# A transformer layer on one core: the opening loads spread over two queues, and the first norm's squares placed behind its last scaled tile

## Chip, core and metric

The kernel runs on one core of one Trainium2 chip. The metric is device time in microseconds (us) of one execution. Five engines work beside each other, each through its own instructions in order: PE (TensorE, matrix products), DVE (VectorE), ACT (ScalarE), POOL (GpSimd) and SP (SyncE, which here only issues transfers). A transfer can be issued by SP or by ACT; the issuing instruction stands in that engine's order like any other, and whatever follows it there comes after it.

## What is computed

One encoder layer on 512 tokens of width 1024, in float32. The part at the beginning is a normalisation and a gated feed-forward half step:

```python
def rms_norm(x, g):
    y = x * lax.rsqrt(jnp.mean(x * x, axis=-1, keepdims=True) + EPS)
    return y * g

def swiglu(h, w_gate, w_up, w_down):
    return (jax.nn.silu(h @ w_gate) * (h @ w_up)) @ w_down

x = x + 0.5 * swiglu(rms_norm(x, ffn1_norm), ffn1_w_gate, ffn1_w_up, ffn1_w_down)
x = x + token_mixing(rms_norm(x, mix_norm), ...)          # gated linear attention and a short convolution
x = x + memory_cross_attention(rms_norm(x, xattn_norm), rms_norm(mem, mem_norm), ...)
x = x + 0.5 * swiglu(rms_norm(x, ffn2_norm), ffn2_w_gate, ffn2_w_up, ffn2_w_down)
out = rms_norm(x, final_norm)
```

The feed-forward width is 2816, so gate and up have 22 tiles of 128 columns each.

## The kernel before

The residual is held transposed, as eight tiles `x[0..7]` of 128 channels by 512 tokens (256 KB each). A norm is split in two: `Norm.scale(d)` multiplies tile d by the gain at once, and the factor 1/rms is multiplied in later, where the products leave PSUM. To keep float32 accuracy each operand of a product is held as a high part and a low part, and a product takes three matmuls (L69 to L71: high by high, high by low, low by high). ACT makes the high part and DVE the low part: of an activation tile in `scaled_split` (`xh` L123, `xl` L124), of a weight unit in `wsplit` (`whi` L65, `wlo` L66). A weight unit is one tile of 128 columns over all 1024 rows, 128x1024 or 512 KB; `ga0`, `ua0`, `ga1`, `ua1` are the first two tiles of gate and up of the first half step. Raw units have four buffers, their high and low parts three each.

The feed-forward loop over f (22 steps, L241) accumulates `pg` (gate) and `pu` (up) over the eight tiles k of the residual, 24 matmuls each. For f = 0 the order is k by k, gate and up in turn, since the tiles arrive one after the other; from f = 1 on it is all of gate, then all of up. The order in which the instructions of an engine finally stand is set by a scheduler from the order in the program and from priorities; the weight units loaded through `unit` have a priority ahead of it.

At the start SP issues everything (`first_units`, L201): residual tiles and quarters of `ga0` and `ua0` (128x256, two k each) in turn, and the scheduler puts `ga1` and `ua1` whole in between. ACT and DVE split them in the same turn.

The sum of squares of the first norm is formed beside that: ACT squares each tile (`Norm.square`, L178: tile 0 into `ssq_n`, L180, the others into `sq_n`, L183, which has two buffers), and POOL adds each square to `ssq_n` (L184, seven adds of 128x512). At f = 2 four small matmuls `rt_n` turn `ssq_n` into the mean over channels, and `rstd_n` comes from it; only then can `finish` empty the banks of f = 0, 1 and 2.

Every transfer signals one of eight semaphores, taken in turn; the ninth transfer's issue waits until the first has landed, and so on. Such waits are named `DMAHW0` to `DMAHW7` below.

Of the kernel before, what the change touches and what calls it, by code (L numbers as in the profile page):

```python
# [15 lines left out]
P = 128  # L16
T = 512
D = 1024
# [12 lines left out]
def layer_kernel(ctx: ExitStack, tc: tile.TileContext, t: dict, outT: bass.AP):  # L31
# [19 lines left out]

# [1 line left out]
    def unit(src, n, name):  # L53
# [19 lines left out]

    # small products, one at a time between the large ones, so that their weights load behind those
    pend = []
# [9 lines left out]
    def mm_cols(ps, w, x, ks, first=True, last=True, tok=slice(0, T)):  # L85
        """ps += the columns of unit w times x; ks: pairs (tile of the unit, tile of x)."""
        whi, wlo = w
        for n, (kw, kx) in enumerate(ks):
            c = slice(kw * P, (kw + 1) * P)
            mm3(ps, whi[:, c], wlo[:, c], x[kx][0][:, tok], x[kx][1][:, tok],  # L90
                first and n == 0, last and n == len(ks) - 1)

    ALL = [(k, k) for k in range(KD)]

# [1 line left out]
    ones = const.tile([P, P], F32, name="ones")  # L96
    nc.gpsimd.memset(ones, 1.0)
    mhalf = const.tile([P, 4], F32, name="mhalf")
    nc.gpsimd.memset(mhalf, -0.5)
    # load the first table and raise the PE's clock while the first tiles are on their way  # L100
    first_table = small.tile([P, 4], F32, tag="warm", name="first_table", bufs=1)
# [20 lines left out]
    def scaled_split(src, g, hi, lo):  # L122
        nc.scalar.activation(hi, src, AF.Copy, scale=g)  # L123
        nc.vector.scalar_tensor_tensor(lo, src, g, hi.bitcast(F32), ALU.mult, ALU.subtract)  # L124

# [1 line left out]
    def rstd_tok(sq, n, width, name):  # L127
        """[128 tokens, n]: the token on the partitions; sq: the tile, or tiles that add up."""
        ps = bank(f"rt_{name}")
        r = small.tile([P, n], F32, tag="rt", name=f"r_{name}", bufs=3)  # L130

        def one(i, m):
            nc.tensor.matmul(ps[:, i:i + 1], lhsT=sq[m][:, i * P:(i + 1) * P], rhs=ones[:, 0:1],
                             start=(i == 0 and m == 0), stop=(i == n - 1 and m == len(sq) - 1), skip_group_check=True)

        def rest():
            ms = small.tile([P, n], F32, tag="ms", name=f"ms_{name}")
            nc.vector.tensor_scalar(ms, ps[:, 0:n], 1.0 / width, EPS, ALU.mult, ALU.add)
            nc.gpsimd.tensor_tensor(r, ms, mhalf[:, 0:n], ALU.pow)

        todo = [[lambda i=i, m=m: one(i, m) for i in range(n)] for m in range(len(sq))]
        todo[-1].append(rest)
        return r, todo

    def spread(r, n, name, parts=2):
        """[128, n * 128] in PSUM: the token on the free axis, the same on every partition."""
        flush()
# [19 lines left out]
    class Norm:  # L167
        """x * gain goes on, split, at once; the factor 1 / rms follows where the products leave PSUM."""

# [4 lines left out]
        def scale(self, d):  # L174
            if self.gi != GFIN:
                scaled_split(x[d], gains[:, self.gi, d:d + 1], xs[d][0], xs[d][1])

        def square(self, d):  # L178
            if d == 0:
                nc.scalar.activation(self.ssq, x[d], AF.Square)  # L180
            else:
                sq = tmp.tile([P, T], F32, tag="sq", name=f"sq_{self.name}{d}", bufs=2)
                nc.scalar.activation(sq, x[d], AF.Square)  # L183
                nc.gpsimd.tensor_tensor(self.ssq, self.ssq, sq, ALU.add)  # L184

        def add(self, d):
# [13 lines left out]

# [1 line left out]
    DOWN = ((0, 8), (8, 15), (15, KF))  # L202

    def first_units(wgu, norm):
        """the first two units and the residual, in the order in which the products need them"""
        g, u = unit(None, D, "ga0"), unit(None, D, "ua0")
        for k in range(0, KD, 2):
            c = slice(k * P, (k + 2) * P)
            for d in (k, k + 1):
                nc.sync.dma_start(x[d], t["xT"][d * P:(d + 1) * P, :])  # L210
                if d == k:
                    nc.sync.dma_start(g[0][:, c], wgu[0, 0][:, c])
                else:
                    nc.sync.dma_start(u[0][:, c], wgu[0, 1][:, c])
        for k in range(0, KD, 2):
            c = slice(k * P, (k + 2) * P)
            norm.scale(k)
            wsplit(*g, c)
            wsplit(*u, c)
            norm.scale(k + 1)  # L220
        return g[1:], u[1:]

    def ffn(wgu, wd, norm, nxt, name, first=None):
# [18 lines left out]
        for f in range(KF):  # L242
            pg, pu = bank(f"pg_{name}{f}"), bank(f"pu_{name}{f}")
            if f == 0 and first is not None:
                g, u = first
                for k in range(KD):
                    mm_cols(pg, g, xs, [(k, k)], k == 0, k == KD - 1)
                    mm_cols(pu, u, xs, [(k, k)], k == 0, k == KD - 1)
                for d in range(KD):
                    norm.square(d)  # L250
            else:
                if f == wait:
                    norm.tok()
                mm_cols(pg, unit(wgu[f, 0], D, f"g{name}{f}"), xs, ALL)
                flush()
                mm_cols(pu, unit(wgu[f, 1], D, f"u{name}{f}"), xs, ALL)
                if f == wait:
                    rstd = norm.rows()
            waiting.append((f, pg, pu))
            if rstd is not None:  # L260
                for w in waiting:
                    finish(*w)
                waiting = []
# [12 lines left out]
    def finale(us, hs):  # L276
        """the last tile of the residual and the last norm, in halves of the tokens"""
        last = KD - 1
# [4 lines left out]
        for i, tok in enumerate(toks):  # L283
            # the residual times the gain, two tiles of it side by side
            y = [tmp.tile([P, T], F32, tag=("fa", "fb", "fs", "fh")[d], name=f"y{d}_{i}") for d in range(KD // 2)]
# [37 lines left out]

# [1 line left out]
    win = t["win"]  # L325
# [23 lines left out]

    # masks over [m, c] of 128 tokens: same chunk and c >= m (forward), c <= m (backward)  # L350
    mf = const.tile([P, P], F32, name="mf")
# [6 lines left out]
    nc.gpsimd.memset(mb[64:128, 0:64], 0.0)  # L358
    # 0 where a chunk's running sum starts anew
    rst = big("rst")  # L360
# [3 lines left out]

    # v and z, tokens on partitions: first columns 0..255 of v, then the others and z
    VK = {0: (256, 4), 1: (288, 3)}
# [35 lines left out]
    def qk(dst, key, j, sc):  # L402
        """each head on both halves of the partitions: forward, backward"""
        ps = bank(f"{key}ps{j}")
# [17 lines left out]

    # gates: rows 0..63 of a head's tile forward, rows 64..127 backward
    lgs, ts = [], []
    for h in range(H):
# [8 lines left out]
        ts.append(ta)  # L434
    # one function at a time: each change of function loads a table
    exps = [nc.scalar.activation(ts[h], ts[h], AF.Exp, scale=-1.0) for h in range(H)]
# [35 lines left out]

# [1 line left out]
    FW, BW = slice(0, 64), slice(64, 128)  # L474
    osn = [None] * H

    def gla(h):
# [33 lines left out]
        for i in range(4):  # L511
            c = slice(i * P, (i + 1) * P)
            for half, r in enumerate((FW, BW)):
                nc.tensor.matmul(aps[half][:, c], lhsT=kin[h][r, c], rhs=qin[h][r, c],
                                 start=(i == 0), stop=(i == 3), skip_group_check=True)
        # the forward triangle over the backward one, the diagonal with the sum of both
        def put(mask, src):
# [39 lines left out]

# [1 line left out]
    rstd2 = big("rstd2")  # L559
# [26 lines left out]

# [1 line left out]
    mk = []  # L588
# [59 lines left out]
    def skewed(gens, lag):  # L648
        """steps of successive generators, each started lag steps after the one before"""
        gens, live, n = list(gens), [], 0  # L650
# [48 lines left out]

# [1 line left out]
    sc = small.tile([P, 4], F32, tag="sc", name="sc", bufs=1)  # L701
# [95 lines left out]

# [1 line left out]
    nf = Norm(GFIN, "nf")  # L799
# [4 lines left out]
def _cols(w):  # L804
    """[K, N] -> [N / 128, 128, K]: a unit is a tile of columns, K in tiles of 128 partitions."""
    k, n = w.shape
    return w.reshape(k // P, P, n // P, P).transpose(2, 1, 0, 3).reshape(n // P, P, k)


def _rows(w, g):  # L810
    """[K, N] -> [K / (128 g), 128, g N]: a unit is g tiles of rows."""
    k, n = w.shape
# [51 lines left out]
```

## Time and profile before

| | us |
|---|---|
| median of 3 runs | 1152.45 (1152.05 to 1152.57) |
| span of the profiled execution, first to last instruction | 1150.4 |
| what lies around that span, against the median | 2.05 |
| PE busy | 1118.1 (97%) |
| PEld (weight loads, beside PE) busy | 934.3 (81%) |
| DVE busy | 576.9 (50%) |
| ACT busy | 392.0 (34%) |
| POOL busy | 173.9 (15%) |

For the profiled execution only its span is given; the runs' times also hold what lies before the first and behind the last instruction. Times of rows below count from the span's start. A busy share is an average over stages with different limits: what the beginning is worth has to be read from the beginning.

### The profile page before, as it was taken

Reading aid. Unit: us, or ns where it says so; the run is one execution under the profiler, and the core shown is the slowest. Engines: PE = TensorE matmul, PEld = TensorE weight load, DVE = VectorE, ACT = ScalarE, POOL = GpSimd, SP = SyncE. Lnnn points to the kernel's source line nnn. Section 1 sums busy time; section 2 is a strip of 40 time slices with the busy share of each in tenths; the row PEclk is TensorE's granted clock in tenths of the full one; section 3 lists DMA queues with packets and bytes.
Section 4 is the critical chain, followed back from the end, with each engine's and each line's share of the span. In section 5 each row is a group of like instructions: output and inputs, shape, how many; then the busy total and the mean of one; then the engine's idle time right before and its main releaser. Section 6 shows DMA issues by size and latency. Waiting matters only on the chain.

```text
span 1150.4 us, 13140 instructions
## 1 busy us (share of the span) xinstructions
PE 1118.1 (97%) x5326; PEld 934.3 (81%) x5326; DVE 576.9 (50%) x735; ACT 392.0 (34%) x549; POOL 173.9 (15%) x145
## 2 busy tenths in 40 slices
PE   8999999999999997798999999999999999999997
PEld 6888888888888986687887888888888888888886
DVE  6455455442333459855767445464555455442223
ACT  6332332322223284322334344353332332232221
POOL 4111111010111027211111300031111011000110
PEclk9999999999999999999999999999999999999998
DMA  6322222323333312311333322032222322323312
GB/s 218 113 95 98 100 92 94 106 85 101 101 95 124 109 56 64 101 56 57 128 104 117 105 79 74 19 128 92 92 92 93 109 92 92 105 83 101 101 51 74
DMA packets 34252, 109.08 MB, mean 95 GB/s; under 512 B 4080, under 2 KB 7152, under 8 KB 34192
## 3 DMA queue, kind: packets, MB, share of 16 engines
q1 hardware_dynamic: 34048, 108.23, 28.8%
q8 instruction: 41, 0.67, 0.2%
q14 instruction: 19, 0.16, 0.0%
q10 hardware_dynamic: 144, 0.02, 0.0%
HBM read 106.14 MB, written 2.10 MB: 94 GB/s over the span
## 4 chain that ended last, share of the span: by engine, by line
PE 86%; DVE 7%; issue 3%; ACT 1%; POOL 1%; DMA 1%; SPq 0%; POOLq 0%; DVEq 0%; ACTq 0%
PE pg_b L69 4%; PE pg_b L71 3%; PE pd_a L69 3%; PE pu_b L71 3%; PE pu_b L69 3%; PE pg_b L70 3%; PE pd_a L71 3%; PE pd_a L70 3%; PE pu_b L70 3%; PE pu_a L71 3%; PE pu_a L70 3%; PE pu_a L69 3%; PE pg_a L69 3%; PE pg_a L70 3%; PE pg_a L71 3%
## 5 line engine op out<-in xcount | busy, mean ns | idle before, releaser
L71 PE MATMUL pu_a<-xh,wlo_ua 128*128 128x512 f32 x176 | 68.7, 390 | 1.3 <-DVE wlo_ua L66 1.3
L71 PE MATMUL pg_a<-xh,wlo_ga 128*128 128x512 f32 x176 | 68.7, 391 | 0.6 <-DVE wlo_ga L66 0.6
L69 PE MATMUL pg_a<-xh,whi_ga 128*128 128x512 f32 x176 | 69.2, 395 | 0.0
L70 PE MATMUL pg_a<-xl,whi_ga 128*128 128x512 f32 x176 | 68.9, 392 | 0.1
L69 PE MATMUL pg_b<-xh,whi_gb 128*128 128x512 f32 x176 | 68.8, 391 | 0.0
L69 PE MATMUL pu_a<-xh,whi_ua 128*128 128x512 f32 x176 | 68.6, 390 | 0.0
L70 PE MATMUL pg_b<-xl,whi_gb 128*128 128x512 f32 x176 | 68.5, 389 | 0.0
L70 PE MATMUL pu_a<-xl,whi_ua 128*128 128x512 f32 x176 | 68.5, 389 | 0.0
L71 PE MATMUL pg_b<-xh,wlo_gb 128*128 128x512 f32 x176 | 68.5, 389 | 0.0
L71 PE MATMUL pu_b<-xh,wlo_ub 128*128 128x512 f32 x176 | 68.5, 389 | 0.0
L69 PE MATMUL pd_a<-hh_a,whi_da 128*128 128x512 f32 x176 | 68.5, 389 | 0.0
L70 PE MATMUL pd_a<-hl_a,whi_da 128*128 128x512 f32 x176 | 68.5, 389 | 0.0
L71 PE MATMUL pd_a<-hh_a,wlo_da 128*128 128x512 f32 x176 | 68.5, 389 | 0.0
L69 PE MATMUL pu_b<-xh,whi_ub 128*128 128x512 f32 x176 | 68.5, 389 | 0.0
L70 PE MATMUL pu_b<-xl,whi_ub 128*128 128x512 f32 x176 | 68.5, 389 | 0.0
L69 PE MATMUL pd_b<-hh_b,whi_db 128*128 128x512 f32 x154 | 59.9, 389 | 0.0
L70 PE MATMUL pd_b<-hl_b,whi_db 128*128 128x512 f32 x154 | 59.9, 389 | 0.0
L71 PE MATMUL pd_b<-hh_b,wlo_db 128*128 128x512 f32 x154 | 59.9, 389 | 0.0
L235 POOL TENSOR_TENSOR fh_a<-fs_a,fb_a 128x512 f32<-128x512 f32 x22 | 30.8, 1402 | 186.5 <-DVE fb_a L233 155.6
L235 POOL TENSOR_TENSOR fh_b<-fs_b,fb_b 128x512 f32<-128x512 f32 x22 | 28.4, 1292 | 198.9 <-DVE fb_b L233 182.2
L66 DVE TENSOR_TENSOR wlo_db<-raw_db,whi_db 128x896 fp32r<-128x896 f32 (+1 forms) x24 | 29.3, 1220 | 54.8 <-ACT whi_db L65 54.2
L66 DVE TENSOR_TENSOR wlo_da<-raw_da,whi_da 128x896 fp32r<-128x896 f32 (+1 forms) x24 | 28.4, 1182 | 49.8 <-ACT whi_da L65 49.1
(361 smaller groups left out, 2773.3 us busy)
## 6 DMA issues: line engine op xcount, KB each, us to landing
raw_gb<-in_w2gu SPq DMA_DIRECT2D x22, 512.0 KB, 3.5
raw_ub<-in_w2gu SPq DMA_DIRECT2D x22, 512.0 KB, 3.4
raw_ga<-in_w1gu SPq DMA_DIRECT2D x21, 512.0 KB, 3.5
raw_ua<-in_w1gu SPq DMA_DIRECT2D x21, 512.0 KB, 3.4
raw_da<-in_w1d SPq DMA_DIRECT2D x16, 448.0 KB, 3.3
raw_db<-in_w2d SPq DMA_DIRECT2D x16, 448.0 KB, 3.2
raw_da<-in_w1d SPq DMA_DIRECT2D x8, 512.0 KB, 3.5
raw_wk<-in_wk SPq DMA_DIRECT2D x8, 512.0 KB, 3.6
```

What stands on the lines that cost most here:

```text
L66: nc.vector.tensor_tensor(lo[:, c], raw[:, c], hi[:, c].bitcast(F32), ALU.subtract)
L69: nc.tensor.matmul(ps, lhsT=whi, rhs=xhi, start=start, stop=False)
L70: nc.tensor.matmul(ps, lhsT=whi, rhs=xlo, start=False, stop=False)
L71: nc.tensor.matmul(ps, lhsT=wlo, rhs=xhi, start=False, stop=stop)
L235: nc.gpsimd.tensor_tensor(h, s, b, ALU.mult)
```

## The change

- `first_units` now opens `ga0`, `ua0`, `ga1` and `ua1` itself and lets ACT issue their loads: first the two heads (columns for k = 0 and 1, 128x256), then the two rests (128x768), then `ga1` and `ua1` whole. All of them are written ahead of ACT's first split.
- SP loads the eight residual tiles one after the other, with nothing between them.
- The splits are written in a new order: tile 0, both heads, tiles 1 and 2, both rests, tiles 3 and 4, `ga1`, tiles 5 and 6, `ua1`, tile 7.
- f = 1 uses the units opened here and is written k by k like f = 0.
- The eight squares are all tied behind the last scaled split (`xh` of tile 7) in ACT's order.

```diff
     def scaled_split(src, g, hi, lo):
-        nc.scalar.activation(hi, src, AF.Copy, scale=g)
+        i = nc.scalar.activation(hi, src, AF.Copy, scale=g)
         nc.vector.scalar_tensor_tensor(lo, src, g, hi.bitcast(F32), ALU.mult, ALU.subtract)
+        return i
...
-        def square(self, d):
+        def square(self, d, behind=None):
             if d == 0:
-                nc.scalar.activation(self.ssq, x[d], AF.Square)
+                i = nc.scalar.activation(self.ssq, x[d], AF.Square)
             else:
                 sq = tmp.tile([P, T], F32, tag="sq", name=f"sq_{self.name}{d}", bufs=2)
-                nc.scalar.activation(sq, x[d], AF.Square)
+                i = nc.scalar.activation(sq, x[d], AF.Square)
                 nc.gpsimd.tensor_tensor(self.ssq, self.ssq, sq, ALU.add)
+            if behind is not None:
+                after(i, behind)
...
     def first_units(wgu, norm):
-        g, u = unit(None, D, "ga0"), unit(None, D, "ua0")
-        for k in range(0, KD, 2):
-            c = slice(k * P, (k + 2) * P)
-            for d in (k, k + 1):
-                nc.sync.dma_start(x[d], t["xT"][d * P:(d + 1) * P, :])
-                if d == k:
-                    nc.sync.dma_start(g[0][:, c], wgu[0, 0][:, c])
-                else:
-                    nc.sync.dma_start(u[0][:, c], wgu[0, 1][:, c])
-        for k in range(0, KD, 2):
-            c = slice(k * P, (k + 2) * P)
-            norm.scale(k)
-            wsplit(*g, c)
-            wsplit(*u, c)
-            norm.scale(k + 1)
-        return g[1:], u[1:]
+        units = [unit(None, D, n) for n in ("ga0", "ua0", "ga1", "ua1")]
+        head = slice(0, 2 * P)
+        rest = slice(2 * P, D)
+        for c in (head, rest):
+            for n in range(2):
+                nc.scalar.dma_start(units[n][0][:, c], wgu[0, n][:, c])
+        for d in range(KD):
+            nc.sync.dma_start(x[d], t["xT"][d * P:(d + 1) * P, :])
+        for n in range(2):
+            nc.scalar.dma_start(units[2 + n][0], wgu[1, n])
+        norm.scale(0)
+        for n in range(2):
+            wsplit(*units[n], head)
+        norm.scale(1)
+        norm.scale(2)
+        for n in range(2):
+            wsplit(*units[n], rest)
+        for d in range(3, KD):
+            norm.scale(d)
+            if d in (4, 6):
+                wsplit(*units[d // 2], slice(0, D))
+        return [u[1:] for u in units]
...
-            if f == 0 and first is not None:
-                g, u = first
+            if f < 2 and first is not None:
+                g, u = first[2 * f:2 * f + 2]
                 for k in range(KD):
                     mm_cols(pg, g, xs, [(k, k)], k == 0, k == KD - 1)
                     mm_cols(pu, u, xs, [(k, k)], k == 0, k == KD - 1)
-                for d in range(KD):
-                    norm.square(d)
+                if f == 0:
+                    for d in range(KD):
+                        norm.square(d, norm.scaled)
```

What the scheduler makes of it differs from the program's order, so three places are shown as the engines get them. From f = 2 on, the instructions of every engine stand in the same order as before.

**ACT, the first instructions.** Before, from the end of the warm-up (`onesr`) on:

```order
L107 ACTIVATE onesr_93<-ones_76 128x128
L123 ACTIVATE xh0_111<-x0_103,gains_100 128x512 [waits DMAHW1_49,DMAHW0_49]
L65 ACTIVATE whi_ga0_130<-raw_ga0_129 128x256 [waits DMAHW2_49]
L180 ACTIVATE ssq_n1_128<-x0_103 128x512
L123 ACTIVATE xh1_113<-x1_104,gains_100 128x512 [waits DMAHW3_49]
```

Now, from the same instruction on:

```order
L107 ACTIVATE onesr_93<-ones_76 128x128
L214 DMA raw_ga0_129<-in_w1gu 128x256
L214 DMA raw_ua0_132<-in_w1gu 128x256
L214 DMA raw_ga0_129<-in_w1gu 128x768 [waits DMAHW0_49]
L214 DMA raw_ua0_132<-in_w1gu 128x768 [waits DMAHW2_49]
L218 DMA raw_ga1_135<-in_w1gu 128x1024 [waits DMAHW5_49]
L218 DMA raw_ua1_138<-in_w1gu 128x1024 [waits DMAHW0_49]
L123 ACTIVATE xh0_111<-x0_103,gains_100 128x512 [waits DMAHW1_49]
L65 ACTIVATE whi_ga0_130<-raw_ga0_129 128x256 [waits DMAHW4_49]
L65 ACTIVATE whi_ua0_133<-raw_ua0_132 128x256 [waits DMAHW6_49]
```

Six issues now stand ahead of the first split, four of them with a wait of their own: by the turn of the eight semaphores these are the landings of the gains, of `x1`, of `x3` and, for `ua1`, of the rest of `ga0`.

**ACT, the squares and the split of `ua1`.** Before, the last residual tile and what follows:

```order
L123 ACTIVATE xh7_125<-x7_110,gains_100 128x512 [waits DMAHW2_49]
L65 ACTIVATE whi_ua0_133<-raw_ua0_132 128x256 [waits DMAHW3_49]
L183 ACTIVATE sq_n17_253<-x7_110 128x512 [waits Pool_49]
L65 ACTIVATE whi_ua1_289<-raw_ua1_288 128x1024 [waits PE_49]
L65 ACTIVATE whi_ga2_323<-raw_ga2_322 128x1024 [waits DMAHW5_49,DVE_49,PE_49]
```

Now, from the last residual tile on:

```order
L123 ACTIVATE xh7_125<-x7_110,gains_100 128x512 [waits DMAHW4_49]
L181 ACTIVATE ssq_n1_128<-x0_103 128x512
L184 ACTIVATE sq_n11_235<-x1_104 128x512
L184 ACTIVATE sq_n12_238<-x2_105 128x512
L184 ACTIVATE sq_n13_241<-x3_106 128x512 [waits Pool_49]
L184 ACTIVATE sq_n14_244<-x4_107 128x512 [waits Pool_49]
L184 ACTIVATE sq_n15_247<-x5_108 128x512 [waits Pool_49]
L184 ACTIVATE sq_n16_250<-x6_109 128x512 [waits Pool_49]
L184 ACTIVATE sq_n17_253<-x7_110 128x512 [waits Pool_49]
L65 ACTIVATE whi_ua1_139<-raw_ua1_138 128x1024 [waits DMAHW0_49,PE_49]
```

All eight squares, five of them waiting for POOL to release one of the two `sq_n` buffers, now stand in one piece between the last residual tile and the split of `ua1`; `ga1` (row not shown) is split before the piece, between tiles 4 and 5.

**PE, f = 1.** Before, the end of gate and the beginning of up:

```order
L70 MATMUL pg_a1_256<-xl7_126,whi_ga1_259 128x512
L71 MATMUL pg_a1_256<-xh7_125,wlo_ga1_260 128x512
L69 MATMUL pu_a1_257<-xh0_111,whi_ua1_289 128x512 [waits Activation_49]
L70 MATMUL pu_a1_257<-xl0_112,whi_ua1_289 128x512
L71 MATMUL pu_a1_257<-xh0_111,wlo_ua1_290 128x512 [waits DVE_49]
L69 MATMUL pu_a1_257<-xh1_113,whi_ua1_289 128x512
```

Now, from the first matmul of f = 1 on, which follows the last one of f = 0:

```order
L69 MATMUL pg_a1_256<-xh0_111,whi_ga1_136 128x512
L70 MATMUL pg_a1_256<-xl0_112,whi_ga1_136 128x512
L71 MATMUL pg_a1_256<-xh0_111,wlo_ga1_137 128x512
L69 MATMUL pu_a1_257<-xh0_111,whi_ua1_139 128x512 [waits Activation_49]
L70 MATMUL pu_a1_257<-xl0_112,whi_ua1_139 128x512
L69 MATMUL pg_a1_256<-xh1_113,whi_ga1_136 128x512
L70 MATMUL pg_a1_256<-xl1_114,whi_ga1_136 128x512
L71 MATMUL pu_a1_257<-xh0_111,wlo_ua1_140 128x512 [waits DVE_49]
L71 MATMUL pg_a1_256<-xh1_113,wlo_ga1_137 128x512
```

Gate and up of f = 1 now alternate from the first tile on: the fourth matmul of f = 1 already needs the high part of `ua1` and the eighth its low part, and 41 of the 48 matmuls stand from that eighth on. Before, the gate products of f = 1 stood among and behind those of f = 0, and the 24 of up came last.

## Rows read from the trace of the kernel before

**Rows 1.** The page: span, and PE's busy time (share, instructions).

```profile
span 1150.4 us, 13140 instructions
PE 1118.1 (97%) x5326; PEld 934.3 (81%) x5326; DVE 576.9 (50%) x735; ACT 392.0 (34%) x549; POOL 173.9 (15%) x145
```

**Rows 2.** Windows: stretch, length, busy per engine, granted clock, DMA share, GB/s.

```profile
0.00:5.00 5.00, 3.95 (x18) 3.95 (x19) 0.22 (x1) 2.66 (x6) 1.01 (x9) 1.00 0.54 155
5.00:10.00 5.00, 4.76 (x18) 3.03 (x16) 2.95 (x5) 3.27 (x7) 2.53 (x4) 1.00 1.02 378
5.30:32.03 26.73, 24.80 (x99) 17.92 (x99) 18.59 (x20) 14.97 (x27) 11.94 (x12) 1.00 0.68 231
```

**Rows 3.** PE in order of time: start, duration; up of f = 1, first of f = 2.

```profile
27.04 0.39 PE L71 MATMUL pu_a<-xh,wlo_ua 128*128 128x512 f32 x1
...
31.80 0.39 PE L71 MATMUL pu_a<-xh,wlo_ua 128*128 128x512 f32 x1
32.03 0.39 PE L69 MATMUL pg_a<-xh,whi_ga 128*128 128x512 f32 x1
```

**Rows 4.** ACT and its issues in order of time, up to the first split.

```profile
0.79 0.40 ACTq L318 DMA_DIRECT2D gains<-in_gains  x1
...
2.63 0.29 ACT L107 ACTIVATE onesr<-ones 128x128 fp32r<-128x128 f32 x1
4.03 0.72 ACT L123 ACTIVATE xh<-x,gains 128x512 fp32r<-128x512 f32 x1 [1.11 <-DMA gains<-in_gains]
```

**Rows 5.** DMA issues of 0.7 to 1.2 us, then one transfer in the chain.

```profile
x<-in_xT SPq DMA_DIRECT2D x1, 256.0 KB, 3.0
gains<-in_gains ACTq DMA_DIRECT2D x1, 24.0 KB, 3.2
...
2.67 5.23 DMA raw_ga<-in_w1gu
```

**Rows 6.** ACT in order of time, the end of the opening.

```profile
16.39 0.72 ACT L123 ACTIVATE xh<-x,gains 128x512 fp32r<-128x512 f32 x1
17.02 0.40 ACT L65 ACTIVATE whi_ga<-raw_ga 128x256 fp32r<-128x256 f32 x1
17.32 0.62 ACT L183 ACTIVATE sq_n<-x 128x512 f32<-128x512 f32 x1
17.84 0.71 ACT L123 ACTIVATE xh<-x,gains 128x512 fp32r<-128x512 f32 x1
...
23.84 1.06 ACT L65 ACTIVATE whi_ua<-raw_ua 128x1024 fp32r<-128x1024 f32 x1 [4.46 <-PE pg_a L70]
24.81 1.04 ACT L65 ACTIVATE whi_ga<-raw_ga 128x1024 fp32r<-128x1024 f32 x1
```

**Rows 7.** POOL's adds: two runs of three in time, then min/median/max in ns.

```profile
11.63 4.41 POOL L184 TENSOR_TENSOR ssq_n<-ssq_n,sq_n 128x512 f32<-128x512 f32 x3 [0.88 <-ACT sq_n L183]
16.52 4.68 POOL L184 TENSOR_TENSOR ssq_n<-ssq_n,sq_n 128x512 f32<-128x512 f32 x3 [0.48 <-ACT sq_n L183]
...
L184 POOL TENSOR_TENSOR ssq_n<-ssq_n,sq_n x7: 1291/1361/1620, 7.5 to 19.9; 128x512 f32<-128x512 f32 x7
```

**Rows 8.** DVE in order of time.

```profile
16.51 0.41 DVE L66 TENSOR_TENSOR wlo_ga<-raw_ga,whi_ga 128x256 fp32r<-128x256 f32 x1
...
18.55 1.51 DVE L66 TENSOR_TENSOR wlo_ua<-raw_ua,whi_ua 128x256 fp32r<-128x256 f32 x1
...
24.93 1.23 DVE L66 TENSOR_TENSOR wlo_ua<-raw_ua,whi_ua 128x1024 fp32r<-128x1024 f32 x1 [1.84 <-PE pu_a L71]
```

**Rows 9.** PE in order of time, later in the kernel, around two idle stretches.

```profile
450.47 0.79 PE L71 MATMUL xps<-xh,wlo_wx 128*128 128x512 f32 x1 [3.58 <-DVE wlo_wx L66]
...
484.54 2.04 PE L530 MATMUL ops<-att,v 128*128 128x128 f32 x8 [5.54 <-DVE att L518]
```

**Rows 10.** Windows of those stretches (granted clock behind POOL's share).

```profile
450.00:453.40 3.40, 2.93 (x7) 2.35 (x8) 3.37 (x4) 0.21 (x1) 1.55 (x1) 0.51 0.49 152
484.00:494.50 10.50, 9.96 (x36) 8.96 (x37) 4.59 (x7) 1.81 (x3) 0.00 (x0) 0.51 0.21 73
```

More of the change, by code (lines that the diff above doesn't have):

```diff
@@ L175, in scale @@
             if self.gi != GFIN:
-                scaled_split(x[d], gains[:, self.gi, d:d + 1], xs[d][0], xs[d][1])
-        def square(self, d):
+                self.scaled = scaled_split(x[d], gains[:, self.gi, d:d + 1], xs[d][0], xs[d][1])
+        def square(self, d, behind=None):
             if d == 0:
-                nc.scalar.activation(self.ssq, x[d], AF.Square)
+                i = nc.scalar.activation(self.ssq, x[d], AF.Square)
             else:
                 sq = tmp.tile([P, T], F32, tag="sq", name=f"sq_{self.name}{d}", bufs=2)
-                nc.scalar.activation(sq, x[d], AF.Square)
+                i = nc.scalar.activation(sq, x[d], AF.Square)
                 nc.gpsimd.tensor_tensor(self.ssq, self.ssq, sq, ALU.add)
+            if behind is not None:
+                after(i, behind)
         def add(self, d):
```

## Prediction

> **What bounds the kernel now.** The page comes first: PE is busy for 97% of the span [rows 1], so time is won or lost only where PE stands still, and what counts is when each stage of PE begins. From f = 2 on every engine has the same instructions in the same order, and PE runs without a gap there; so the effect of the change is, but for its sign, one number: when the first matmul of f = 2 starts. Before, that is 32.03 us [rows 3]. In the stretch up to it PE is busy 24.80 of 26.73 us [rows 2], and the step from one matmul to the next, where nothing is waited for, is (31.80 - 27.04) / 21 = 0.227 us [rows 3]. The 96 matmuls of f = 0 and 1 would take 21.8 us; the opening loses some 5 us, in waits for splits and tiles. That is all that a better opening could win, if it began as early. The reader should then look at ACT and POOL in order of time: ACT starts its first split at 4.03 us [rows 4], and its squares lie between its splits.
>
> **The six issues ahead of ACT's first split.** An issue takes ACT 0.40 us, and the warm-up ends at 2.63 + 0.29 = 2.92 us [rows 4]. Without waits the six would be through at 2.92 + 6 x 0.40 = 5.3 us. But ACT goes in order, and the last one (`ua1`) waits until the rest of `ga0` has landed. When is that? Before, the fifth transfer of SP's queue, `ga1`, was issued at 2.67 and landed 5.23 us later, at 7.90 [rows 5]. With it 1304 KB (1.34 MB) had to move. By the windows 155 GB/s flowed up to 5 us (0.78 MB) and 378 GB/s after that [rows 2], so those bytes had passed at 6.5 us, and the landing came 1.4 us later. I use the same two rates and the same 1.4 us. Which bytes pass ahead of the rest of `ga0` no row shows, since before only the 24 KB of gains went through ACT's queue (they took 3.2 us beside 3.0 us of the 256 KB tile issued with them [rows 5]). Lower bound, ACT's queue served first: gains, `x0`, `x1`, two heads and the rest itself, 1176 KB = 1.20 MB, passed at 6.1, landed 7.6. Upper bound, SP's queue served first: six residual tiles with it, 2200 KB = 2.25 MB, passed at 8.9, landed 10.3. With 0.40 for the last issue, ACT starts `xh0` between 8.0 and 10.7 us; I take the middle, 9.4. Against 4.03 before this is 5.4 us late, and the splits of all tiles, hence DVE and PE, stand behind it.
>
> On this the Trainium skill speaks against the change. Its page "DMA: Bandwidth & Descriptors", section "Issuing engines are not separate DMA queues", says that transfers of all issuing engines run on the same 16 DMA engines and interleave, and that a second issuing engine saves only issue time; section "Queues, rings and completion order" has each DMA engine take turns between queues. Rows moving in equal turns would put `x2`, `x3` beside the heads and `x4` beside the rest, 1944 KB, landed at 9.6, `xh0` at 10.0; by this rule the sum below would be 0.6 us higher. No row of this trace shows two full queues side by side.
>
> **ACT from there to the squares.** Starts follow each other by 0.63 us behind an `xh`, 0.30 behind a 128x256 split, 0.52 behind a square, 0.97 behind a 128x1024 split [rows 6]; for 128x768 I take 0.75, between the last two sizes of split in proportion. Eight `xh` (5.04), two heads (0.60), two rests (1.50) and `ga1` (0.97) make 8.1 us, so the first square starts at 17.5 and the second, the first to be added, ends at 18.05 + 0.62 = 18.7.
>
> **The squares behind the last tile.** There are two `sq_n` buffers, so each square from the fourth on waits for an add, and the eighth waits for the fifth add. Before, this was hidden: squares came a tile at a time. Now the eight stand in one piece, and the split of `ua1` stands behind them on ACT. An add took 1.291 us at its shortest, and 4.41 / 3 = 1.47 or 4.68 / 3 = 1.56 while DVE worked beside it [rows 7]. DVE has little left in that time, so I take 1.29 (upper bound 1.56). The fifth add ends at 18.7 + 6.45 = 25.2, the eighth square starts there, `whi_ua1` 0.52 later at 25.7, and ends 1.06 later [rows 6], at 26.75. Before it started at 23.84, held by PE [rows 6], and two thirds of the work of f = 1 did not need it any more or not yet; now the fourth matmul of f = 1 does.
>
> Then DVE makes `wlo_ua1`, 1.23 us. The seventh add runs to 18.7 + 7 x 1.29 = 27.75 beside it. A 128x256 low part took 0.41 us alone and 1.51 among adds [rows 8]. So a DVE instruction among adds is held; I let `wlo_ua1` wait for the add's end: 27.75 + 1.23 = 29.0. Not held it would be 28.0, the lower bound.
>
> **PE.** f = 0 starts about 1.1 us behind `xh0`, at 10.5, and lasts at least 48 x 0.227 = 10.9 us, to 21.4; three matmuls of f = 1 take it to 22.1. Then it stands until 26.75, does four, and stands until 29.0. Whatever f = 0 loses on the way, up to 4 us, is covered by that wait. The 41 matmuls left take 9.3 us: f = 2 would start at 29.1 + 9.3 = 38.4.
>
> **The clock.** Later in this kernel PE stood for 3.58 us and then did seven matmuls in 2.93 us at a granted clock of 0.51, the lower level of 1.2 GHz, where 7 x 0.227 = 1.6 would do [rows 9, 10]: 1.3 us. Around an idle stretch of 5.54 us the lower clock lasted through a window of 10.5 us [rows 9, 10]; were all of it dense work, half of its 9.96 busy us, 5.0, would be lost. The new gap of 4.6 us lies between the two. I take 1.3, since the short low stretch was followed by dense matmuls as here; bounds 0 and 5.0.
>
> **Moved at no cost.** SP's queue is freed of the units and gives the tiles without pause; ACT needs the last tile only at 9.4 + 7.5 = 16.9, when by the rate of rows 2 more than 3 MB (3072 KB are tiles, `ga0` and `ua0` together) have passed. The units of f = 2 are issued behind them and behind DVE's split of the rests, some 5 us after `xh0`, and are needed at 38. The four low parts saved on DVE (eight small ones become four) are worth under 2 us where DVE is not waited for. The mean of the norm needs the seventh add (27.75), ahead of f = 2.
>
> **Sum.** f = 2 starts at 38.4 + 1.3 = 39.7 instead of 32.03: 7.7 us later. The profiled span of 1150.4 becomes 1158.1; the 2.05 us between it and the median of the runs stay, so 1152.45 + 7.7 = 1160.1 us. All bounds low: 1.4 (queue), 1.0 (`wlo_ua1`) and 1.3 (clock) less, 1156.4. All high: 1.3 (queue), 7 x 0.27 = 1.9 (adds), 3.7 (clock) more, 1167.0, which needs three bad ends at once.
>
> **Rivals.**
> 1. *The waits of ACT's issues cost nothing*, because the landings they name come before ACT gets there. Then `xh0` starts at 5.3, 4.1 us earlier, and all behind it moves along: 1156.0. Against it: no transfer of 384 KB that is issued after 3 us could land by 5, when 24 KB of gains alone took 3.2 us [rows 5].
> 2. *The lower clock lasts*, as around the 5.54 us gap: 3.7 us more, 1163.8. For it: the gap ahead of f = 1 is 4.6 us, and a second one of 1.3 follows.
> 3. *The squares do not hold `ua1`* (the other side). Then PE itself decides, as before: `whi_ua1` can start four matmuls before the end of f = 0, at 20.5, `wlo_ua1` is there at 22.8, and f = 2 starts at 22.9 + 9.3 = 32.2: 1152.6, no change. With `xh0` at 8.0 it would be 1.4 less, 1151.2; to be faster by over 0.2% takes `xh0` before 6.9. It decides if the fifth add ends by 20.0, so at 0.26 us an add; the shortest was 1.29.
>
> **How the numbers follow.** Forecast 0.82 (own range 1156.4 to 1164), rival 1 0.05, rival 2 0.08, rival 3 0.05, of which 0.02 with an early ACT. A measurement of this kernel can tell about 0.2%, 2.3 us. Slower 0.95, same 0.03, faster 0.02. The range that holds 8 in 10 is 1156.0 to 1164.0, the time that of the forecast, 1160.1.
>
> **What would show it.** ACT's first `xh` at 8.0 to 10.7 us, right behind the issue of `ua1`; squares from the fourth on an add apart, released by POOL; `whi_ua1` at once behind the eighth square, at 24 to 28; on PE an idle stretch of 3 us or more in front of the fourth matmul of f = 1, released by ACT, and a shorter one, released by DVE; a granted clock of half in f = 1; f = 2 at 36 to 43 us, and the same distances as before from there to the end. It is wrong if `whi_ua1` is released by PE, if ACT's first split starts before 7, or if the end does not move with the start of f = 2.

## The result and the profile after

The changed kernel takes 1157.75 us (median, 1155.21 to 1159.82 over 6 runs) where the kernel before took 1152.22 beside it; the ratio is 1.0064 with a 95% interval of 1.0044 to 1.0084. Timed once more in a later series (`e10` below) it took 1159.12 us, at a ratio of 1.0074 [1.0052, 1.0096]. It is slower by 5.5 and 8.6 us by these medians, by 7.4 and 8.5 us by the ratios. The forecast was 1160.1 (range 1156.0 to 1164.0), which is 7.7 over the 1152.45 known then.

ACT in order of time, the opening (a row marked ACTq is an issue; in brackets the idle time before a row and what ended it):

```profile
1.31 0.36 ACTq L214 DMA_DIRECT2D raw_ga<-in_w1gu  x1
1.70 0.46 ACTq L214 DMA_DIRECT2D raw_ua<-in_w1gu  x1
2.52 0.20 ACT L102 ACTIVATE first_table<-mhalf 128x4 f32<-128x4 f32 x1
2.63 0.29 ACT L107 ACTIVATE onesr<-ones 128x128 fp32r<-128x128 f32 x1
3.54 0.33 ACTq L214 DMA_DIRECT2D raw_ga<-in_w1gu  x1
5.06 0.34 ACTq L214 DMA_DIRECT2D raw_ua<-in_w1gu  x1
7.22 0.34 ACTq L218 DMA_DIRECT2D raw_ga<-in_w1gu  x1
9.05 0.34 ACTq L218 DMA_DIRECT2D raw_ua<-in_w1gu  x1
9.43 0.72 ACT L123 ACTIVATE xh<-x,gains 128x512 fp32r<-128x512 f32 x1 [6.51 <-DMA x<-in_xT]
```

Against [rows 4], the first split comes at 9.43 instead of 4.03 us. The bracket blames the tile `x0`, but that had long landed, 3.1 us after its issue at 0.80: between the rows there are four issues, each standing 1.5 to 2.2 us behind the one ahead of it, and the split follows the last at once. Issues are not counted as work, so the row of the split shows their waits as its own.

The end of the opening on ACT, then POOL and DVE beside it:

```profile
18.42 0.61 ACT L184 ACTIVATE sq_n<-x 128x512 f32<-128x512 f32 x1
20.30 0.63 ACT L184 ACTIVATE sq_n<-x 128x512 f32<-128x512 f32 x1 [1.26 <-POOL ssq_n L185]
...
25.74 0.63 ACT L184 ACTIVATE sq_n<-x 128x512 f32<-128x512 f32 x1 [0.71 <-POOL ssq_n L185]
26.28 1.04 ACT L65 ACTIVATE whi_ua<-raw_ua 128x1024 fp32r<-128x1024 f32 x1
...
18.67 9.74 POOL L185 TENSOR_TENSOR ssq_n<-ssq_n,sq_n 128x512 f32<-128x512 f32 x7 [16.10 <-ACT sq_n L184]
...
27.35 2.15 DVE L66 TENSOR_TENSOR wlo_ua<-raw_ua,whi_ua 128x1024 fp32r<-128x1024 f32 x1 [8.24 <-ACT whi_ua L65]
29.42 1.21 DVE L66 TENSOR_TENSOR wlo_ga<-raw_ga,whi_ga 128x1024 fp32r<-128x1024 f32 x1
```

In [rows 6] `whi_ua1` waited 4.46 us for PE; now it has no wait of its own and stands directly behind the eighth square, which, like the four before it, waited for an add. POOL is then the engine that sets the pace: seven adds with hardly a pause between them, 18.67 to 28.41.

PE around the hole, and the first matmul of f = 2:

```profile
24.00 0.39 PE L71 MATMUL pg_a<-xh,wlo_ga 128*128 128x512 f32 x1
27.37 0.50 PE L69 MATMUL pu_a<-xh,whi_ua 128*128 128x512 f32 x1 [2.98 <-ACT whi_ua L65]
...
29.55 0.79 PE L71 MATMUL pu_a<-xh,wlo_ua 128*128 128x512 f32 x1 [0.98 <-DVE wlo_ua L66]
30.14 0.63 PE L71 MATMUL pg_a<-xh,wlo_ga 128*128 128x512 f32 x1
30.57 0.63 PE L69 MATMUL pu_a<-xh,whi_ua 128*128 128x512 f32 x1
...
41.66 0.39 PE L69 MATMUL pg_a<-xh,whi_ga 128*128 128x512 f32 x1
```

The two stops stand where the order put them, the first released by ACT, the second by DVE. From 30.14 to 34.84 the matmuls follow each other by 0.43 us and not by 0.227. The windows say why (granted clock behind POOL's share):

```profile
8.03:14.86 6.83, 4.35 (x10) 3.44 (x11) 4.67 (x8) 5.43 (x10) 0.00 (x0) 0.50 0.90 332
28.51:35.34 6.83, 5.85 (x15) 4.54 (x15) 2.13 (x2) 0.00 (x0) 0.00 (x0) 0.50 0.46 156
```

The clock is at its lower level, 1.2 GHz, in both: the first stretch begins within the 5.27 us in which PE waited for the first split, the second at 28.51, in the last of the four matmuls behind the wait of 2.98 us. f = 2 starts at 41.66 instead of 32.03 [rows 3], 9.6 us later.

The profiled span, however, is 1155.2 us, only 4.8 more than before. Followed from split to split, the kernels are 9.6 to 10.8 us apart up to 575 us, but in the end 4.9, so the other 4.8 came back far behind the opening, nearly all at one place. There PE waits equally long in both kernels, for `att` of the attention; rows of PE and the windows from there, first before, then after:

```profile
570.12 1.20 PE L530 MATMUL ops<-att,v 128*128 128x128 f32 x4 [2.73 <-DVE att L518]
...
569.50:579.75 10.25, 9.63 (x45) 9.66 (x46) 3.27 (x6) 1.11 (x3) 0.00 (x0) 0.50 0.34 104
```

```profile
579.47 1.13 PE L540 MATMUL ops<-att,v 128*128 128x128 f32 x8 [2.73 <-DVE att L528]
...
579.50:582.00 2.50, 2.50 (x23) 2.50 (x23) 1.93 (x4) 0.42 (x1) 0.00 (x0) 1.00 0.66 216
```

The same idle 2.73 us were followed by 10.24 us at the lower clock in one execution and by none in the other. Whether that belongs to the change or to the execution is what `e9` and `e10` are for.

### The profile page after: what moved, and what is told of

Read it like the earlier page. It is cut to its first block, busy times and chain, and to the rows that moved or that the text cites. A ratio compares the mean times of both kernels' runs of the same rounds, so it can differ in the third digit from the quotient of the medians.

```text
span 1155.2 us, 13126 instructions
## 1 busy us (share of the span) xinstructions
PE 1116.6 (97%) x5326; PEld 934.5 (81%) x5326; DVE 568.6 (49%) x731; ACT 391.5 (34%) x545; POOL 175.3 (15%) x145
## 3 DMA queue, kind: packets, MB, share of 16 engines
q10 hardware_dynamic: 1008, 2.12, 0.5%
## 4 chain that ended last, share of the span: by engine, by line
PE 85%; DVE 7%; issue 3%; POOL 2%; ACT 2%; DMA 1%; POOLq 0%; DVEq 0%; ACTq 0%
PE pg_b L69 3%; PE pd_a L71 3%; PE pg_b L70 3%; PE pu_b L70 3%; PE pu_b L69 3%; PE pd_a L70 3%; PE pg_b L71 3%; PE pu_b L71 3%; PE pd_a L69 3%; PE pu_a L71 3%; PE pg_a L69 3%; PE pu_a L69 3%; PE pg_a L71 3%; PE pu_a L70 3%; PE pg_a L70 3%
```

## The experiments

My theory: f = 2 starts late because (a) ACT's first split stands behind issues that wait for landings, (b) the squares, two buffers to eight, hold ACT and with it `whi_ua1`, and (c) f = 1 needs `ua1` from its fourth matmul on; what happens behind f = 2 is the clock of one execution. Rivals: the lower clock is the cause and the holes are not; the squares are not what holds `ua1`; the late start itself changes the rest.

Summary, with f = 2's first matmul from the profile (before: 32.03, changed: 41.66):

| run | first split | `whi_ua1` | f = 2 | median us | ratio to before [95%] |
|---|---|---|---|---|---|
| changed kernel | 9.43 | 26.28 | 41.66 | 1157.75 | 1.0064 [1.0044, 1.0084] |
| e1, own buffer per square | 9.89 | 24.09 | 36.80 | 1153.34 | 1.0024 [1.0010, 1.0037] |
| e2, f = 1 all gate first | 9.87 | 26.77 | 35.21 | 1153.35 | 1.0013 [0.9996, 1.0029] |
| e3, `ga1`, `ua1` on SP | 5.54 | 22.99 | 36.08 | 1153.56 | 1.0023 [1.0010, 1.0035] |
| e4, squares between splits | 9.92 | 30.05 | 41.61 | 1160.10 | 1.0085 [1.0062, 1.0109] |
| e5, matmuls in the hole | 9.64 | 26.53 | 39.70 | 1157.05 | 1.0066 [1.0042, 1.0090] |
| e6, before with tied squares | 3.80 | 21.20 | 29.62 | 1150.70 | 0.9994 [0.9977, 1.0011] |
| e7, e6 with own buffers | 3.84 | 21.94 | 30.35 | 1150.93 | 1.0010 [0.9997, 1.0023] |
| e8, e1 + e2 + e3 | 5.42 | 19.70 | 31.14 | 1147.72 | 0.9986 [0.9969, 1.0003] |
| e9, e8 again | 5.68 | 19.36 | 30.83 | 1148.98 | 0.9991 [0.9975, 1.0006] |
| e10, changed again | 10.11 | 26.97 | 41.14 | 1159.12 | 1.0074 [1.0052, 1.0096] |

**e1: the squares' buffers.** The changed kernel, but each square of the first norm has a tile of its own.

```diff
-                sq = tmp.tile([P, T], F32, tag="sq", name=f"sq_{self.name}{d}", bufs=2)
+                if self.name == "n1":
+                    sq = big(f"sq_{self.name}{d}")
+                else:
+                    sq = tmp.tile([P, T], F32, tag="sq", name=f"sq_{self.name}{d}", bufs=2)
```

> The changed kernel with a buffer of its own for each square of the first norm, so that no square waits for an add; the orders on the engines stay. Theory (f = 2 is late because the split of ua1 stands behind squares that wait for adds): the eighth square starts at 21.0 us (17.38 + 7 x 0.52), whi_ua1 is released by PE at about 24.0 and not by a square, wlo_ua1 is there between 26.3 and 27.7 (held by an add for up to 1.4), PE stands under 2 us before it, the granted clock stays up in f = 1, and f = 2 starts at 35.7 to 37.1 instead of 41.66. Rival (PE's late start of 10.5 us alone is what is passed on): f = 2 within 1 us of 41.7.

ACT, then DVE and PE:

```profile
24.09 1.06 ACT L65 ACTIVATE whi_ua<-raw_ua 128x1024 fp32r<-128x1024 f32 x1 [1.99 <-PE pg_a L70]
...
25.19 2.12 DVE L66 TENSOR_TENSOR wlo_ua<-raw_ua,whi_ua 128x1024 fp32r<-128x1024 f32 x1 [5.61 <-ACT whi_ua L65]
...
27.36 0.50 PE L71 MATMUL pu_a<-xh,wlo_ua 128*128 128x512 f32 x1 [0.81 <-DVE wlo_ua L66]
```

PE releases `whi_ua1` again, the hole of 2.98 us is gone, the matmuls of f = 1 behind the short stop follow each other by 0.23 us, and f = 2 starts 4.9 us earlier. So (b) holds. (In f = 0, from 12.05 to 16.74, they still stand 0.43 us apart, as in the changed kernel, although this profile's granted clock reads 1.00 there: the steps tell more than that record.) But f = 2 is still 4.8 us later than before: taking the squares away does not bring back 32.2.

**e2: the order of f = 1.**

```diff
-                for k in range(KD):
-                    mm_cols(pg, g, xs, [(k, k)], k == 0, k == KD - 1)
-                    mm_cols(pu, u, xs, [(k, k)], k == 0, k == KD - 1)
+                if f == 0:
+                    for k in range(KD):
+                        mm_cols(pg, g, xs, [(k, k)], k == 0, k == KD - 1)
+                        mm_cols(pu, u, xs, [(k, k)], k == 0, k == KD - 1)
+                else:
+                    mm_cols(pg, g, xs, ALL)
+                    mm_cols(pu, u, xs, ALL)
```

> The changed kernel with f = 1 as before the change: all of gate, then all of up. Nothing else moves. Theory (the order tile by tile in f = 1 exposes the wait for ua1): ACT and DVE as in the changed kernel (whi_ua1 at 26.3, wlo_ua1 ready at 29.5), but PE does 24 gate products from 24.0 to 29.2 meanwhile, never stands for 1 us, the clock stays up, and f = 2 starts at 34.5 (29.5 + 22 x 0.227). Rival (late start passed on): f = 2 within 1 us of 41.7.

`whi_ua1` is as late as in the changed kernel (26.77) and costs nothing: PE has no idle time over 0.25 us from 10.95 on, does the 24 gate products meanwhile, and f = 2 starts at 35.21, 6.5 us earlier. (c) holds: a late split is only as dear as the order that asks for it.

**e3: the issues.** `ga1` and `ua1` are issued by SP, behind the tiles.

```diff
         for n in range(2):
-            nc.scalar.dma_start(units[2 + n][0], wgu[1, n])
+            nc.sync.dma_start(units[2 + n][0], wgu[1, n])
```

> The changed kernel with ga1 and ua1 issued by SP behind the residual tiles, so that ACT issues four loads instead of six. Theory (ACT's first split waits for the landing of the rest of ga0 only through the last issue): xh0 starts at 5.4 to 6.0 us instead of 9.43, right behind the fourth issue; the tiles from the third on then wait for the rests (landed at 9 to 10.5), the squares begin at about 15.3 instead of 17.38, whi_ua1 starts at about 22.5, and f = 2 at 35 to 38. Rival (the four waits that ACT keeps cost as much): xh0 after 8 us, f = 2 within 1 us of 41.7.

ACT from the two issues that are left on:

```profile
5.16 0.33 ACTq L214 DMA_DIRECT2D raw_ua<-in_w1gu  x1
5.54 0.72 ACT L123 ACTIVATE xh<-x,gains 128x512 fp32r<-128x512 f32 x1 [2.61 <-DMA x<-in_xT]
...
22.46 0.63 ACT L184 ACTIVATE sq_n<-x 128x512 f32<-128x512 f32 x1 [0.71 <-POOL ssq_n L185]
22.99 1.04 ACT L65 ACTIVATE whi_ua<-raw_ua 128x1024 fp32r<-128x1024 f32 x1
23.94 1.04 ACT L65 ACTIVATE whi_ga<-raw_ga 128x1024 fp32r<-128x1024 f32 x1
24.89 0.61 ACT L184 ACTIVATE sq_n<-x 128x512 f32<-128x512 f32 x1
```

Two issues less, and the first split moves by 3.9 us: (a) holds. The rests of `ga0` and `ua0` now hold tile 3 (`xh3` at 11.09), so that the first square comes only 1.7 us earlier (15.69). `whi_ua1` is 3.3 us earlier, and part of that is not the issues: the scheduler now puts the eighth square behind `whi_ua1` and the next split, as the last row shows, so `whi_ua1` waits for one add less, 1.4 us at the steps of the squares. At f = 2 it is 5.6 us; the 2.3 more come for the most part from the lower clock, which follows the hole for 3.41 us and not for 6.83. So the 5.6 us are not the price of the two issues alone.

**e4: the squares' place, a miss.** The squares stand between the splits again, each behind its own tile.

```diff
-        norm.scale(0)
+        norm.add(0)
...
-            norm.scale(d)
+            norm.add(d)
...
-                if f == 0:
-                    for d in range(KD):
-                        norm.square(d, norm.scaled)
```

(`norm.add(d)` is `scale(d)` and `square(d)`.)

> The changed kernel's opening alone: each square directly behind the split of its tile, two square buffers, no tie. Theory (adds hold DVE, squares in one piece hold ACT): DVE's low parts of the tiles take up to 1.8 us again, f = 0 ends later than 24.0, at about 25 to 27, but whi_ua1 is released by PE with its end, and f = 2 starts at 35.5 to 38.5. So the new place of the squares wins time in f = 0 and loses more in f = 1. Rival (the place of the squares does not matter): f = 2 within 1 us of 41.7.

I expected the hold of `ua1` to go and nothing to come for it. DVE and ACT show what came (two and three `xl` in one row):

```profile
17.64 3.47 DVE L124 SCALAR_TENSOR_TENSOR xl<-x,gains,xh 128x512 fp32r<-128x512 f32 x2
...
23.27 4.10 DVE L124 SCALAR_TENSOR_TENSOR xl<-x,gains,xh 128x512 fp32r<-128x512 f32 x3
...
30.05 1.06 ACT L65 ACTIVATE whi_ua<-raw_ua 128x1024 fp32r<-128x1024 f32 x1 [7.13 <-PE pg_a L70]
```

POOL's adds now run among the low parts. An `xl` that took 0.75 us in the changed kernel takes up to 1.78, PE waits for `xl` three times in f = 0 (0.96, 1.79 and 0.27 us), and f = 0, which ended at 24.4 in the changed kernel, runs to about 30: `whi_ua1` waits for PE until 30.05. So the new place of the squares is not simply a loss: it frees DVE in f = 0, where e4 ends some 6 us later (1.0 of it a later start, some 1.5 a second stretch at the lower clock behind those waits), and loses as much in f = 1. This corrects the theory: what costs is not that the squares stand last, but that they stand ahead of `whi_ua1` with two buffers.

**e5: the clock.** Thirteen matmuls of 512 columns are added on PE between f = 0 and f = 1, into a bank that nothing reads, so that the hole is filled with work.

```diff
+                    wp2 = bank("warm2")
+                    for i in range(13):
+                        nc.tensor.matmul(wp2, lhsT=onesr, rhs=xs[KD - 1][0], start=(i == 0), stop=(i == 12))
```

> The changed kernel with 13 added matmuls of 512 columns on PE between f = 0 and f = 1, into a bank that nothing reads: 13 x 0.227 = 3.0 us of work in the 3.0 us in which PE stood. They take no time from f = 1. Theory on the clock (the matmuls of f = 1 ran at half clock because PE had stood): the granted clock stays up from 15 us on, f = 1 loses nothing to it, and f = 2 starts at 38.9 to 39.4 instead of 41.66, still late, since wlo_ua1 is there at 29.5 as before. Rival (the low clock has another cause, or the added work only pushes f = 1): f = 2 at 41.7 or later.

The window in which the changed kernel had half the clock:

```profile
28.51:35.34 6.83, 5.52 (x24) 4.60 (x25) 2.39 (x2) 0.01 (x1) 0.17 (x1) 1.00 0.47 155
```

`wlo_ua1` is ready 0.26 us later than in the changed kernel, yet f = 2 starts at 39.70, 2.0 earlier. From the first matmul with `wlo_ua1` to f = 2 it is 9.88 us (29.82 to 39.70) and not 12.11: the lower clock cost 2.2 us. The time is 1.0066, not to be told from the changed kernel's 1.0064, as 2 us of 1150 would hardly be. f = 2 still starts 7.7 us later than before, so the rival that the clock alone makes the loss falls.

**e6 and e7: the squares' place in the kernel before.** Only the tie of the squares behind the last scaled split is added to the kernel before; e7 also gives each square its own tile, by the diff of e1.

```diff
-                    norm.square(d)
+                    norm.square(d, norm.scaled)
```

> The kernel before with one part of the change alone: its squares tied behind the last scaled split. The scheduler then puts the split of ua1 behind three squares, not eight. Theory: no add holds DVE before 19 us, the low parts of the tiles take 0.75 us each, f = 0 ends at about 20.5 instead of 25, the split of ua1 is released by PE, and f = 2 starts at 28.5 to 30, 2 to 3.5 us earlier than before (32.03); the time falls by 0.2 to 0.3%. Rival (the squares' place costs a wait wherever it stands): f = 2 at 33 to 36.

> As the kernel before with tied squares, and with a buffer of its own for each square. Theory: the splits of the third and fourth weight units no longer stand behind squares that wait for adds, so f = 2 starts as early or up to 1 us earlier than with two buffers, and nothing waits behind f = 2's first matmuls for the sum of squares longer than 1 us. Rival: no difference.

The opening does get shorter: every `xl` takes 0.75 us, `whi_ua1` starts at 21.20, f = 2 at 29.62. But three matmuls later a wait stands that was not there before; PE in e6 and in e7:

```profile
32.61 0.38 PE L134 MATMUL rt_n<-ones,ssq_n 128*128 128x1 f32 x2 [2.15 <-POOL ssq_n L185]
```

```profile
34.23 0.38 PE L134 MATMUL rt_n<-ones,ssq_n 128*128 128x1 f32 x2 [3.04 <-POOL ssq_n L188]
```

The mean over channels needs the seventh add, and that is now the last thing to come. Own buffers, which helped in e1, do not help here. In both kernels adds fall beside the 128x1024 low parts and take 2.12 to 2.16 us instead of 1.29: two of the seven in e6, three in e7, where the seventh is one of them. The wait is 0.9 us longer in e7, and f = 2 0.7 us later; its transfers also landed later (the split of `ga1` starts at 9.26, not 8.53), so no run shows that the buffers are what makes it worse. I expected a gain of 0.2 to 0.3% from e6 and a wait of at most 1 us in e7; the times are those of before. The 2.4 us that e6 had won at f = 2 were taken back but for 0.3 us within three matmuls.

**e8 and e9: the three parts undone or freed together**, the edits of e1, e2 and e3 in one kernel; e9 is the same kernel again.

> The changed kernel with three things taken back or freed at once: ga1 and ua1 issued by SP, eight square buffers, f = 1 gate first. Theory: xh0 at 5.5, f = 0 ends at about 20.5, gate of f = 1 to 26, whi_ua1 released by PE at about 20.5, f = 2 at 31 to 32, as the kernel before; the time within 0.2% of before. Rival (something else of the change costs): f = 2 after 34.

> The kernel with all three edits once more, unchanged, timed again. The start of f = 2 should come within 0.5 us of the first profile's 31.14, since the order is the same. If its first median, 2.6 us under that of before, was a gain of the opening (f = 2 some 0.9 us earlier gives 0.1%), the ratio comes out at 0.998 to 1.000; if it was chance, at 0.999 to 1.002. The two intervals together decide whether it is better than before.

f = 2 starts at 31.14 and 30.83, as expected, and the whole 9.6 us are back. The time does not settle on a gain: 0.9986 and 0.9991, both intervals reaching over 1. It is no worse than before and is not shown to be better: by an estimate from the two intervals, the pair together is at about 0.9989 and reaches just to 1. The three single steps gave 4.9, 6.5 and 5.6 us, 17 in sum, and 10.5 together: they shorten the same hole, so each pays only until the next reason holds.

The pair shows more. Both run one program, their f = 2 start 0.3 us apart, and their spans are 1149.6 and 1143.9. Windows at the same times, e8 then e9:

```profile
527.60:531.00 3.40, 3.15 (x9) 2.04 (x8) 2.41 (x4) 0.37 (x1) 0.77 (x1) 0.50 0.48 157
...
568.60:578.80 10.20, 9.61 (x45) 9.64 (x46) 3.25 (x6) 1.09 (x3) 0.00 (x0) 0.50 0.36 104
```

```profile
527.60:531.00 3.40, 3.40 (x25) 3.05 (x23) 1.09 (x2) 1.49 (x2) 0.00 (x0) 1.00 0.02 5
...
568.60:578.80 10.20, 10.20 (x74) 10.20 (x74) 3.98 (x9) 3.12 (x5) 1.82 (x4) 0.82 0.26 80
```

Followed from split to split, e9 is 0.3 us ahead up to 371 us, 3.3 at 497, 4.4 at 534 and 5.7 from 579 to the end. Nearly all of it lies between 439 and 580 us, where PE waits several times for 1.4 to 5.6 us, and where e8 has 27.3 us at the lower clock and e9 17.1. The runs of the kernel before show such a spread too: the 30 beside e8 took 1146.0 to 1154.1 us, at mean granted clocks of 0.982 to 0.989.

**e10: the changed kernel once more.**

> The changed kernel once more, unchanged. My theory is that f = 2 starts 9.6 us late by the order of the opening, and that the 4.8 us which the first profile had back by the end were stretches at the lower clock that differ from one execution to the next. Then f = 2 starts within 0.5 us of 41.66 again, while stretches at the lower clock stand at other places behind it, and the distance to before at the end is not 4.8 again but anything from 3 to 12 us; the median is 5 to 9 us over before. The rival, that the rest of the kernel gives the 4.8 back because of the late start, has the same places and 4.8 us again within 1.

f = 2 at 41.14, 0.52 from the first profile; at the end 5.9 us behind before (span 1156.3). Three stretches stand at the same waits as in the first profile, at 460, 491 and 535 us, but there is none at 421, and one where the first profile had none, behind the wait for `att`:

```profile
579.50:586.30 6.80, 6.80 (x33) 6.80 (x33) 0.78 (x2) 0.60 (x1) 0.00 (x0) 0.50 0.30 89
```

The distance of 5.9 alone would hardly part the theory from the rival (4.8 within 1), but these two places do, and e8 with e9 shows the same spread in one program with an equal start.

## Why the prediction was right

- **ACT's issues.** Forecast 9.4 (8.0 to 10.7), found 9.43, and 9.43 to 10.11 over the six profiles with this order. The bounds held; that the first profile met the middle of them is chance. The last issue came right behind the landing of the rest of `ga0`, issued at 3.54 and landed at 9.03. The issues ahead of it came differently from the sum, the first at 1.31, while the table was still loading, instead of 2.92; that did not matter, since the landing decides. On the disputed point, the Trainium skill, page "DMA: Bandwidth & Descriptors", section "Queues, rings and completion order", has each DMA engine take turns between the queues, packet by packet. The prediction's other sum, 10.0, took the turns as equal in bytes, and the six profiles have a mean of 9.81, nearer to 10.0 than to 9.4. But the trace agrees only in part. From 3 to 5 us the two queues moved 268 and 277 packets, with 0.48 MB on SP's queue and 0.25 MB on ACT's; from 5 to 7 us it was 339 packets beside 26, although the rest of `ga0` had been issued at 3.54. So neither queue was served first throughout, nor did they share equally, and the 9.81 does not show the rule.
- **The squares.** Forecast: first square 17.5, fifth add ends 25.2, eighth square there, `whi_ua1` at 25.7, or 27.0 by the upper bound of the adds. Found: 17.38, 25.71, 25.74 and 26.28. The adds were mis-sized by little: 9.74 / 7 = 1.39 us a step with the pause between two adds, not 1.29.
- **The low part.** That `wlo_ua1` waits for the last add held: 2.15 us beside it, 1.21 for the next one alone. The Trainium skill, page "SBUF — State Buffer", section "Who interferes with whom", says that a VectorE instruction with two inputs in SBUF contends with a GpSimd one that reads SBUF, and that the ports they share are held under an exclusive lock. The trace agrees in both directions: in e7 it was also the adds that went from 1.29 to 2.16.
- **f = 0.** Forecast to end at 21.4 at the least, found 24.4 with the three matmuls of f = 1 (22.1 forecast). Ten of its matmuls ran at the lower clock, behind the wait for ACT, which I had not counted. As written, the hole covered it, so it did not move f = 2; PE's idle time was shorter by it, 2.98 and not 4.6 us (2.60 in e10), just under the 3 us that I had named as a sign. It does count in rival 3, whose 1152.6 was too low: without the hold, in e1, f = 2 starts at 36.8, not at 32.2 (0.5 us from a later start, some 2.9 from f = 0 at the lower step, 1.0 from the stop before `wlo_ua1`), and the time is 2.3 us over before by the medians.
- **The clock.** Forecast 1.3 us (0 to 5.0). Thirteen steps from 29.55 to 35.27 took 5.72 us where 2.95 would do: 2.8 us lost. By e5 it is 2.2, and e10 had only 3.41 us at the lower clock and 10.89 us from 30.25 to f = 2, 1.6 over the 9.3 of full clock. This term was the largest error of the sum.
- **The sum.** f = 2 came 9.6 us late (9.1 in e10), forecast 7.7: 1.5 from the clock, 0.45 from `wlo_ua1`.
- **To the end.** Here the prediction's reading was too simple. It took the distance at f = 2 for the distance at the end; in one execution the clock elsewhere moved the end by 4.8 us, which is as much as half the effect. Over several runs the medians came back to 5.5 and 8.6 us, the ratios to 7.4 and 8.5. So the forecast time was nearly met in part by luck: the start came 1.9 us later than forecast, and the end followed it by 1 to 2 us less. That shortfall itself is not clear of the noise, since the two intervals are 5.1 to 9.7 and 6.0 to 11.0 us and both hold the 9.6. e1, e2 and e3 also lie 1.4 to 2.0 us under their shift of f = 2, clearly so only e1 (1.2 to 4.3 us by its interval, for 4.8); e4 and e5 do not (9.8 us for 9.6, 7.6 for 7.7). Whether there is a shortfall, and whether it belongs to the late start or to where the one profile of before stands in its spread, stays open.

## What to carry to other kernels

A load issued on an engine that computes is an instruction of that engine: if its semaphore is shared with an earlier load, everything behind it waits for that landing, and the trace shows the wait under the next instruction's name. Moving work to the end of an engine's queue is only free if what stands behind it there is needed later still, and if its consumers (here POOL with two buffers, then DVE and the mean) are not the next ones to be late; ask for each moved piece who is last now. Several reasons for one hole don't add up: undone singly they gave 17 us, together 10.5.

## What the runs showed of the hardware

- One program, twice: spans of 1143.9 and 1149.6 us, with 25.6 and 34.9 us of them at the lower clock. The same wait of 2.73 us before `att` was followed by 10.24 us at 1.2 GHz, by 6.83 or by none, in executions of two kernels. An effect under some 5 us can't be read from the span of one profile of this kernel; the start of a stage near the change can.
- Issues on ACT went out while its table was still being loaded (1.31 and 1.70 us beside a load from 1.22 to 2.50).
- With loads on both queues, 365 GB/s flowed from 3 to 5 us and 332 from 8.03 to 14.86 in the changed kernel, no more than the 378 of [rows 2] with nearly all on SP's queue; a load of 384 KB took 5.4 to 5.5 us to land.
